# Three 256-column products into one sum, where a 512-column and a 256-column product made two sums

## The chip, the cores and the metric

The kernel runs on one core of a Trainium2 chip. The metric is the device time of one execution in microseconds (us). Engines are named as the profile names them: PE is TensorE's products (MATMUL), PEld its weight loads (LDWEIGHTS), DVE is VectorE, ACT is ScalarE, POOL is GpSimd and SP is SyncE, which issues most DMAs.

## What is computed

One decoder layer on 256 tokens of width 2048, in float32. A projection to seven parts feeds an attention branch and a recurrent branch; each branch is projected and gated, the sum is projected again, and a gated feed-forward part of width 5632 follows. Cut to its matrix products:

```python
def hybrid_layer(x, ...):
    h = rms_norm(x, norm1_w)
    q, k, v, xr, yr, g_att, g_lru = jnp.split(h @ w_in, SPLIT_POINTS, axis=-1)
    att = moba_attention(rms_norm(q), rms_norm(k), v)
    lru = rglru_branch(xr, yr, ...)
    merged = (jax.nn.sigmoid(g_att) * (att @ w_proj_attn)
              + jax.nn.sigmoid(g_lru) * (lru @ w_proj_lru))
    x = x + merged @ w_out
    h2 = rms_norm(x, norm2_w)
    return x + (jax.nn.silu(h2 @ w_ffn_gate) * (h2 @ w_ffn_up)) @ w_ffn_down
```

## The kernel before

All weights together are a list of 292 pieces of 512 rows x 512 columns (1 MB each), used one after the other in the order in which `plan` was filled. SP fetches a piece three ahead of its use (`load`). `split` makes two parts of every piece, each in two halves of 256 rows: ACT rounds it to `w_hi` (L107) and DVE subtracts to get the rest, `w_lo` (L108). There are four buffers of halves for each part, so that two pieces are held at a time, and a half is written again when TensorE has used it for the last time. The left operands (`hT`, `attT`, `lruT`, `merged`, `h2T`, `mid`) are held in two parts in the same way, as [128, part, 4, 256]. A product of x and w is made of three: high by high, high by low, low by high.

A block is 512 columns of one projection, 4 pieces long (11 in the last projection, `fd`). The 12 blocks of q, k and v (48 pieces) keep the activations stationary (`tokens_first`: L648, L649, L650, three products of 512 columns for each 128 rows and half of the tokens, each with its own weight load, though two follow each other with the same stationary operand). The other 244 pieces keep the weights stationary (`features_first`). For each of the 4 groups of 128 rows (k) and 4 groups of 128 columns (f), a block of `w_hi` is loaded and meets both parts of the activations in one product of 512 columns (L661; the two parts lie 1024 elements apart, so the operand is read in two runs of 256), and then a block of `w_lo` is loaded and meets the high part in one of 256 columns (L662). These are pairs of products; there are 16 in a piece and 3904 in all. A block's two sums are two PSUM tiles `acc[g]`, one for each two f; `gather` copies one sum out with ACT (L304) and adds the other with DVE (L305), half a block per piece, and then the work of the block's kind follows (multiplying by the row's 1/rms, gates, residual sums).

The order on each engine is the order of the program: behind each piece `run_due` issues the tasks that are due (`later(delay, ...)` counts in pieces), at most one of them for TensorE. `aux` products of these tasks (attention scores, transposes, recurrent gates) stand between pieces. The last piece of all goes one f at a time, in the order 0, 2, 1, 3, and `last_evac` adds and stores each f behind it.

Of the kernel before, what the change touches and what calls it, by code (L numbers as in the profile page):

```python
# [23 lines left out]
CB = 512          # columns of one block of a projection  # L24
KT = 4            # chunks of 128 rows in one loaded piece of a weight
# [5 lines left out]
# columns of `vecs`, 16 each (feature = column * 128 + partition)  # L31
# [6 lines left out]
def layer(ctx: ExitStack, tc: tile.TileContext, x, xT, vecs, w_in, w_rg_a, w_rg_x,  # L38
# [18 lines left out]
    pieces = []     # (source, first row chunk, first column)  # L57
# [5 lines left out]
    plan = []       # (kind, index, source of the left operand)  # L63
# [28 lines left out]
    def load(n):  # L92
        if n >= len(pieces):
            return
        w, k, c = pieces[n]
        raw[n] = wp.tile([P, KT, CB], F32, name="w_raw", bufs=4)
        src = w[k * P:(k + KT) * P, c:c + CB].rearrange("(k p) n -> p k n", p=P)
        if n == 0:
            return src
        if n > 1:  # L100
            sync.dma_start(raw[n], src)
        else:
            for s in range(0, KT, 2):
                sync.dma_start(raw[n][:, s:s + 2], src[:, s:s + 2])
# [49 lines left out]
    # the first pieces come chunk by chunk, so that TensorE starts early  # L154
# [16 lines left out]
    # identity, distances  # L171
# [17 lines left out]
    def rsqrt_mean(name, ss, n, width, where=small):  # L189
        """(ss / n + EPS) ** -0.5"""  # L190
        r = where.tile([P, width], F32, name=name)
        pool.tensor_scalar(r, ss, 1.0 / n, EPS, op0=OP.mult, op1=OP.add)
        pool.tensor_tensor(r, r, mhalf[:, :width], op=OP.pow)
        return r
# [3 lines left out]
    def rows_of(r):  # L198
        """[token, half] -> [128 times the same, token]: a task for TensorE, then a copy"""
        box = const.tile([P, T], F32, name="rb")  # L200

        def on_pe():
            t = aux()
            for h in range(2):
                pe.transpose(t[:, h * P:(h + 1) * P], r[:, h:h + 1].to_broadcast([P, P]), ident)
            later(1, lambda: act.activation(box, t[:, :T], AF.Copy))
        later(1, on_pe, True)
        return box

# [31 lines left out]
    # softplus(-lambda) = max(-lambda, 0) + 2 atanh(e / (2 + e)), e = exp(-|lambda|)  # L241
# [23 lines left out]
    tasks = []      # [slot, order, on TensorE, function]  # L265
# [20 lines left out]
    def transposed(src):  # L286
        """[token, half, 512 features] -> PSUM [feature, 4, token]"""
        t = aux()
        tv = t.rearrange("p (k h t) -> p k h t", k=KT, h=2)
        for k in range(KT):  # L290
            for h in range(2):
                pe.transpose(tv[:, k, h, :], src[:, h, k * P:(k + 1) * P], ident)  # L292
        return t

    def parts_of(dst, src):
        """dst [128, 2, 4, 256] from src [128, 4, 256]"""
        act.activation(dst[:, 0], src, AF.Copy)
        later(1, lambda: dve.tensor_tensor(dst[:, 1], src, dst[:, 0].bitcast(F32), op=OP.subtract))

    def gather(acc, dst, then):  # L300
        """dst [128, 4, 256] from the two sums of each feature"""
        def half(g):
            d = dst[:, 2 * g:2 * g + 2]
            act.activation(d, acc[g][:, :, 1, :], AF.Copy)  # L304
            dve.tensor_tensor(d, acc[g][:, :, 0, :], d, op=OP.add)  # L305
        later(0, lambda: half(0))
        later(1, lambda: (half(1), then()))
# [55 lines left out]
    def scores(b):  # L363
# [44 lines left out]
        def turn(z, pair):  # L408
            t = aux().rearrange("p (a n) -> p a n", a=2)
            for a in range(2):  # L410
                hd = 2 * pair + a
                # keys of the first half: queries of both halves; keys of the second: queries of it
                pe.transpose(t[:, a, :P], z[:, hd, :P], ident)  # L413
                pe.transpose(t[:, a, P:2 * P], z[:, hd, P:2 * P], ident)  # L414
                pe.transpose(t[:, a, 2 * P:3 * P], z[:, hd, 2 * P:], ident)  # L415

            def after():
                if pair == 0:
                    box["pT"] = arena.tile([P, KT, 3 * P], F32, name="pT", tag="m7")
                act.activation(box["pT"][:, 2 * pair:2 * pair + 2], t[:, :, :3 * P], AF.Copy)  # L420
                if pair == 1:
                    later(0, values, True)
            later(1, after)
# [22 lines left out]
    sg = {}  # L446

    def gate_of(s, delay=1):
        dve.tensor_tensor(s, s, rows(st["rb1"]), op=OP.mult)
        later(delay, lambda: act.activation(s, s, AF.Sigmoid))  # L450

    def ga_done(j, acc):
        if j % 2 == 0:
            sg["pair"] = arena.tile([P, 2, KT, T], F32, name="s", tag=f"m{8 + j // 2}")
        sg[j] = sg["pair"][:, j % 2]
        gather(acc, sg[j], lambda: gate_of(sg[j]))

    def pa_done(j, acc):
        t = feat_tile(f"t{j % 2}", "pa")
        gather(acc, t, lambda: dve.tensor_tensor(sg[j], t, sg[j], op=OP.mult))  # L460

    def gl_done(j, acc):
# [5 lines left out]
        gather(acc, s, lambda: gate_of(s, 2))  # L468

    def pl_done(j, acc):  # L470
        t = feat_tile(f"t{j % 2 * 2}", "pl")

        def then():
            dve.tensor_tensor(t, t, sg["l", j], op=OP.mult)
# [3 lines left out]
        gather(acc, t, then)  # L478

# [1 line left out]
    lru = {}  # L481

    def xr_done(b, acc):
# [12 lines left out]
        def scaled():  # L496
            dve.tensor_tensor(xv, xv, rows(st["rb1"]), op=OP.mult)
            conv(0)
            later(1, lambda: conv(1))
# [37 lines left out]
        def factor(g, at):  # L537
            # 1 - a^2 = tanh(-log a) (1 + a^2)
# [10 lines left out]
        gather(acc, xv, scaled)  # L549

    def yr_done(b, acc):
        s = feat_tile("t2", "yr")

        def then():
            dve.tensor_tensor(s, s, rows(st["rb1"]), op=OP.mult)
            later(2, lambda: act.activation(s, s, AF.Gelu_apprx_tanh))
            later(5, product)
# [5 lines left out]
        gather(acc, s, then)  # L563

# [9 lines left out]
    def add(xb, acc, f):  # L574
        for s in (1, 0):
            dve.tensor_tensor(xb[:, f], acc[f.start // 2][:, f.start % 2:(f.stop - 1) % 2 + 1, s, :],
                              xb[:, f], op=OP.add)

    def wo_done(j, acc):
        xb = res[j]  # L580

        def then():
            add(xb, acc, slice(2, 4))
# [7 lines left out]
        later(0, lambda: add(xb, acc, slice(0, 2)))  # L591
        later(1, then)

# [1 line left out]
    ff = {}  # L595

    def fg_done(j, acc):
        g = feat_tile(f"t{j % 2}", "fg")

        def scaled():  # L600
            s = feat_tile("t2", "fs")
            dve.tensor_tensor(g, g, rows(st["rb2"]), op=OP.mult)
# [6 lines left out]
        gather(acc, g, lambda: later(3 if j == 0 else 0, scaled))  # L609

    def fu_done(j, acc):
        u = feat_tile("t3", "fu")

        def scaled():
            dve.tensor_tensor(u, u, rows(st["rb2"]), op=OP.mult)
# [3 lines left out]
        gather(acc, u, lambda: later(2 if j == 0 else 0, scaled))  # L619

    def fd_done(j, acc):
        xb = res[j]

        def then():
            add(xb, acc, slice(2, 4))
            sync.dma_start(out_rows[:, j * KT:(j + 1) * KT], xb)
        later(0, lambda: add(xb, acc, slice(0, 2)))
        later(1, then)
# [12 lines left out]
    def tokens_first(acc, a, n, first, last):  # L641
        """acc [token, half, column]: the left operand's parts are stationary"""
# [9 lines left out]
    def features_first(acc, a, n, first, last, fs=range(KT)):  # L652
        """acc[g] [column, 2, 2, token]: the weight's parts are stationary; its first part meets both parts
        of the activations in one product, and the two sums are added in the end"""
        for g in range(2):
            mine = [(k, f) for k in range(KT) for f in fs if f // 2 == g]
            for k, f in mine:
                hi, lo = (p[:, k % 2, f * P:(f + 1) * P] for p in parts[n][k // 2])
                o = acc[g][:, f % 2]
                start, stop = first and k == 0, last and k == KT - 1  # L660
                pe.matmul(o, hi, a[:, :, k, :], start=start, stop=False, skip_group_check=True)  # L661
                pe.matmul(o[:, 0, :], lo, a[:, 0, k, :], start=False, stop=stop, skip_group_check=True)  # L662

    for kind, j, n0, count in plan:
# [3 lines left out]
        else:  # L668
            acc = [psum.tile([P, 2, 2, T], F32, name="acc", tag="acc", bufs=3) for g in range(2)]
# [70 lines left out]
```

## Time and profile before

| | |
|---|---|
| median of 3 runs (1688.47 to 1690.04) | 1689.32 us |
| span of the profiled execution, first to last instruction | 1686.6 us |
| PE / PEld busy | 1676.7 / 1455.4 us |
| DVE / ACT busy | 1040.0 / 827.9 us |
| granted TensorE clock, mean | 1.000 |
| DMA, mean over the span | 190 GB/s |

The time that lies around the span is taken as 1689.3 - 1686.6 = 2.7 us; the profiled execution has no other time than its span. A product's duration in the trace reaches from its start to the end of its last result, so that products overlap, and their rhythm has to be read from start to start, or from the busy time of a group divided by its count where products of the group cover its whole stretch.

### The profile page before, as it was taken

To read this page: it belongs to the slowest core of one execution; us is meant where nothing else is said; L and a number is where in the kernel's file an instruction comes from. 1 tells how busy PE (TensorE), PEld (TensorE's weight loads), DVE (VectorE), ACT (ScalarE), POOL (GpSimd) and SP (SyncE) were. 2 spreads that over 40 slices of the span, in tenths; PEclk is the share of its full clock that TensorE was granted. 3 is DMA by queue.
4 is the path that set the end of the run, shared out by engine and by line. 5 is a ranking of instruction groups with operands and counts; after the bars stand their busy time and mean duration, and the time that the engine had idled before them with its cause. 6 is when DMAs were issued, how large, how long until landed. Compare 5 with 4: busy or idle time off the path is not lost.

```text
span 1686.6 us, 22468 instructions
## 1 busy us (share of the span) xinstructions
PE 1676.7 (99%) x9276; PEld 1455.4 (86%) x9276; DVE 1040.0 (62%) x1064; ACT 827.9 (49%) x960; POOL 27.7 (2%) x35
## 2 busy tenths in 40 slices
PE   8999999999999999999999999999999999999999
PEld 6888888888888888888888888888888888888887
DVE  6565656655556867768666656666666666554444
ACT  6544554544445665756445444444444444443332
POOL 0100101000000000000000000000000000000000
PEclk9999999999999999999999999999999999999999
DMA  8554545555555555555557655555556555565662
GB/s 306 190 179 155 177 169 174 170 173 182 190 198 175 187 184 203 187 175 177 198 188 245 216 189 186 200 180 194 192 184 199 181 193 192 184 223 188 213 218 82
DMA packets 166294, 320.30 MB, mean 190 GB/s; under 512 B 5296, under 2 KB 15664, under 8 KB 166192
## 3 DMA queue, kind: packets, MB, share of 16 engines
q1 hardware_dynamic: 165328, 316.51, 55.6%
q0 software_dynamic: 576, 2.10, 0.3%
q8 instruction: 72, 1.18, 0.3%
q10 hardware_dynamic: 288, 0.26, 0.0%
q14 instruction: 30, 0.25, 0.0%
HBM read 314.66 MB, written 4.19 MB: 189 GB/s over the span
## 4 chain that ended last, share of the span: by engine, by line
PE 99%; DMA 0%; ACT 0%; SPq 0%; DVE 0%; issue 0%
PE acc L661 53%; PE acc L662 27%; PE acc L649 5%; PE acc L650 5%; PE acc L648 5%; PE aux L515 1%; PE aux L292 0%; PE aux L372 0%; PE aux L431 0%; DMA xc<-in_xT 0%; PE aux L433 0%; PE aux L371 0%; PE aux L415 0%; PE aux L413 0%; PE aux L414 0%; SPq L158 0%
## 5 line engine op out<-in xcount | busy, mean ns | idle before, releaser
L108 DVE TENSOR_TENSOR w_lo<-w_raw,w_hi 128x1024 fp32r<-128x1024 f32 (+1 forms) x586 | 711.9, 1221 | 575.8 <-ACT w_hi L107 575.7
L107 ACT ACTIVATE w_hi<-w_raw 128x1024 fp32r<-128x1024 f32 (+1 forms) x586 | 619.0, 1058 | 757.0 <-PE acc L661 548.5
L661 PE MATMUL acc<-h2T,w_hi 128*128 128x512 f32 x1408 | 488.9, 392 | 0.0
L662 PE MATMUL acc<-h2T,w_lo 128*128 128x256 f32 x1408 | 394.3, 280 | 0.0
L661 PE MATMUL acc<-hT,w_hi 128*128 128x512 f32 x1024 | 360.9, 397 | 0.0
L661 PEld LDWEIGHTS acc<-h2T,w_hi 128*128 128x128 f32 x1408 | 263.4, 187 | 58.1
L662 PE MATMUL acc<-hT,w_lo 128*128 128x256 f32 x1024 | 286.3, 280 | 0.0
L662 PEld LDWEIGHTS acc<-h2T,w_lo 128*128 128x128 f32 x1408 | 266.1, 189 | 0.0
L661 PE MATMUL acc<-mid,w_hi 128*128 128x512 f32 x704 | 244.1, 391 | 0.0
L661 PEld LDWEIGHTS acc<-hT,w_hi 128*128 128x128 f32 x1024 | 192.1, 188 | 45.2
L662 PE MATMUL acc<-mid,w_lo 128*128 128x256 f32 x704 | 197.1, 280 | 0.0
L662 PEld LDWEIGHTS acc<-hT,w_lo 128*128 128x128 f32 x1024 | 193.2, 189 | 0.3
L648 PE MATMUL acc<-w_hi,hT 128*128 128x512 f32 x384 | 153.9, 401 | 5.5 <-ACT w_hi L107 5.4
L661 PEld LDWEIGHTS acc<-mid,w_hi 128*128 128x128 f32 x704 | 131.6, 187 | 28.9
L649 PE MATMUL acc<-w_lo,hT 128*128 128x512 f32 x384 | 151.0, 393 | 0.8 <-DVE w_lo L108 0.8
L650 PE MATMUL acc<-w_hi,hT 128*128 128x512 f32 x384 | 150.7, 392 | 0.0
L662 PEld LDWEIGHTS acc<-mid,w_lo 128*128 128x128 f32 x704 | 133.1, 189 | 0.0
L648 PEld LDWEIGHTS acc<-w_hi,hT 128*128 128x128 f32 x384 | 72.8, 190 | 20.9 <-ACT w_hi L107 6.5
L661 PE MATMUL acc<-attT,w_hi 128*128 128x512 f32 x256 | 90.5, 399 | 0.0
L661 PE MATMUL acc<-merged,w_hi 128*128 128x512 f32 x256 | 90.5, 399 | 0.0
L661 PE MATMUL acc<-lruT,w_hi 128*128 128x512 f32 x256 | 90.3, 398 | 0.1
L649 PEld LDWEIGHTS acc<-w_lo,hT 128*128 128x128 f32 x384 | 72.7, 189 | 16.5 <-DVE w_lo L108 2.0
(166 smaller groups left out, 1303.8 us busy)
## 6 DMA issues: line engine op xcount, KB each, us to landing
w_raw<-in_w_in SPq DMA_DIRECT2D x110, 1024.0 KB, 5.0
w_raw<-in_w_ffn_gate SPq DMA_DIRECT2D x44, 1024.0 KB, 5.0
w_raw<-in_w_ffn_up SPq DMA_DIRECT2D x44, 1024.0 KB, 5.0
w_raw<-in_w_ffn_down SPq DMA_DIRECT2D x44, 1024.0 KB, 5.0
w_raw<-in_w_proj_attn SPq DMA_DIRECT2D x16, 1024.0 KB, 5.0
w_raw<-in_w_proj_lru SPq DMA_DIRECT2D x16, 1024.0 KB, 4.9
w_raw<-in_w_out SPq DMA_DIRECT2D x16, 1024.0 KB, 5.1
xb<-in_xT SPq DMA_DIRECT2D x4, 512.0 KB, 7.9
```

The costliest lines, as they stand in the source:

```text
L107: act.activation(hi, r, AF.Copy)
L108: dve.tensor_tensor(lo, r, hi.bitcast(F32), op=OP.subtract)
L515: pe.matmul(t[:, n * T:(n + 1) * T], wg[:, i, n, :], u[:, n, :], start=True, stop=True, skip_group_check=True)
L648: pe.matmul(o, ah, hi, start=(first and k == 0), stop=False)
L649: pe.matmul(o, ah, lo, start=False, stop=False)
L650: pe.matmul(o, al, hi, start=False, stop=(last and k == KT - 1))
L661: pe.matmul(o, hi, a[:, :, k, :], start=start, stop=False, skip_group_check=True)
L662: pe.matmul(o[:, 0, :], lo, a[:, 0, k, :], start=False, stop=stop, skip_group_check=True)
```

## The change

`features_first` makes three products of 256 columns for each k and f, all into one sum: `w_hi` by the high part, `w_hi` by the low part, `w_lo` by the high part. Its loops are exchanged: f is outside, k inside. A block's sums fit one PSUM tile `acc` of two banks, and `gather` is gone. In its place `by_rows` reads the tile with one DVE instruction, which multiplies by the row's 1/rms in the same pass; the residual sums take one addition for a block in place of four. Delays of tasks are set for this. In DRAM every weight lies piece by piece, with a partition's 4 x 512 numbers of a piece in one run of 8 KB, where there were four runs of 2 KB in four rows.

```diff
-        src = w[k * P:(k + KT) * P, c:c + CB].rearrange("(k p) n -> p k n", p=P)
+        src = w[k // KT, c // CB]
...
-    def gather(acc, dst, then):
-        """dst [128, 4, 256] from the two sums of each feature"""
-        def half(g):
-            d = dst[:, 2 * g:2 * g + 2]
-            act.activation(d, acc[g][:, :, 1, :], AF.Copy)
-            dve.tensor_tensor(d, acc[g][:, :, 0, :], d, op=OP.add)
-        later(0, lambda: half(0))
-        later(1, lambda: (half(1), then()))
+    def by_rows(acc, dst, r, then, delay=0):
+
+        def fn():
+            dve.tensor_tensor(dst, acc, rows(st[r]), op=OP.mult)
+            then()
+        later(delay, fn)
...
     def add(xb, acc, f):
-        for s in (1, 0):
-            dve.tensor_tensor(xb[:, f], acc[f.start // 2][:, f.start % 2:(f.stop - 1) % 2 + 1, s, :],
-                              xb[:, f], op=OP.add)
+        dve.tensor_tensor(xb[:, f], acc[:, f], xb[:, f], op=OP.add)
...
             later(1, lambda: parts_of(mid[j], u))
-        gather(acc, u, lambda: later(2 if j == 0 else 0, scaled))
+        by_rows(acc, u, "rb2", lambda: later(3, scaled), 1 if j == 0 else 0)
...
-        for g in range(2):
-            mine = [(k, f) for k in range(KT) for f in fs if f // 2 == g]
-            for k, f in mine:
+
+
+        for f in fs:
+            for k in range(KT):
                 hi, lo = (p[:, k % 2, f * P:(f + 1) * P] for p in parts[n][k // 2])
-                o = acc[g][:, f % 2]
-                start, stop = first and k == 0, last and k == KT - 1
-                pe.matmul(o, hi, a[:, :, k, :], start=start, stop=False, skip_group_check=True)
-                pe.matmul(o[:, 0, :], lo, a[:, 0, k, :], start=False, stop=stop, skip_group_check=True)
+                o = acc[:, f, :]
+                start, stop = first and k == 0 and f % 2 == 0, last and k == KT - 1
+                pe.matmul(o, hi, a[:, 0, k, :], start=start, stop=False, skip_group_check=True)
+                pe.matmul(o, hi, a[:, 1, k, :], start=False, stop=False, skip_group_check=True)
+                pe.matmul(o, lo, a[:, 0, k, :], start=False, stop=stop, skip_group_check=True)
...
-            acc = [psum.tile([P, 2, 2, T], F32, name="acc", tag="acc", bufs=3) for g in range(2)]
+            acc = psum.tile([P, KT, T], F32, name="acc", tag="acc", bufs=3)
...
+        if not k.startswith("w_rg"):
+            rows_, cols_ = given[k].shape
+            given[k] = (given[k].reshape(rows_ // (KT * P), KT, P, cols_ // CB, CB)
+                        .transpose(0, 3, 2, 1, 4))
```

Line numbers move: the three products of `features_first` are L648, L649 and L650 of the changed kernel. On TensorE's queue, in a features-first piece of the attention gate's projection where the piece's second half is used for the first time, before (`acc_2222` is the PSUM tile of f = 0 and 1, the numbered `w_hi` and `w_lo` are halves of the piece):

```order
L661 MATMUL acc_2222<-hT_84,w_hi_2302 128x512
L662 MATMUL acc_2222<-hT_84,w_lo_2303 128x256
L661 MATMUL acc_2222<-hT_84,w_hi_2306 128x512
L662 MATMUL acc_2222<-hT_84,w_lo_2307 128x256
L661 MATMUL acc_2222<-hT_84,w_hi_2306 128x512
```

The same place in the changed kernel (`acc_2222` is now the tile of the whole block; the numbers of halves differ):

```order
L648 MATMUL acc_2222<-hT_84,w_hi_2317 128x256
L649 MATMUL acc_2222<-hT_84,w_hi_2317 128x256
L650 MATMUL acc_2222<-hT_84,w_lo_2318 128x256
L648 MATMUL acc_2222<-hT_84,w_hi_2321 128x256
L649 MATMUL acc_2222<-hT_84,w_hi_2321 128x256
L650 MATMUL acc_2222<-hT_84,w_lo_2322 128x256
```

Where two products stood for a k and an f, three stand now, and the second half of the piece's rows is used for the first time after 6 products (of 48), where it was after 8 (of 32). The whole TensorE queue has 3904 rows more.

In the last piece, on TensorE's queue with its waits, the changed kernel has at the end of f = 0 and the beginning of f = 2:

```order
L649 MATMUL acc_16409<-mid_14652,w_hi_16934 128x256
L650 MATMUL acc_16409<-mid_14652,w_lo_16935 128x256
L648 MATMUL acc_16409<-mid_14652,w_hi_16930 128x256 [waits DVE_49]
L649 MATMUL acc_16409<-mid_14652,w_hi_16930 128x256
L650 MATMUL acc_16409<-mid_14652,w_lo_16931 128x256
```

Before, that place read (f = 2 has a tile of its own, and only the third and the fourth f wait for DVE):

```order
L661 MATMUL acc_12940<-mid_11613,w_hi_13325 128x512
L662 MATMUL acc_12940<-mid_11613,w_lo_13326 128x256
L661 MATMUL acc_12941<-mid_11613,w_hi_13321 128x512
L662 MATMUL acc_12941<-mid_11613,w_lo_13322 128x256
L661 MATMUL acc_12941<-mid_11613,w_hi_13321 128x512
```

All four f now lie in one tile, so each of the last three waits for the DVE addition of the f just before it; before, an f waited for the addition of the one two before it.

On DVE, over a gate block and an up block of the feed-forward part, before:

```order
L305 TENSOR_TENSOR fg<-acc,fg 128x512
L298 TENSOR_TENSOR mid<-fu,mid 128x1024
L108 TENSOR_TENSOR w_lo<-w_raw,w_hi 128x1024 x2
L602 TENSOR_TENSOR fg<-fg,rb 128x1024
L108 TENSOR_TENSOR w_lo<-w_raw,w_hi 128x1024 x4
L607 TENSOR_TENSOR fg<-fg,fs 128x1024
L305 TENSOR_TENSOR fu<-acc,fu 128x512
```

The same blocks in the changed kernel:

```order
L303 TENSOR_TENSOR fg<-acc,rb 128x1024
L108 TENSOR_TENSOR w_lo<-w_raw,w_hi 128x1024 x4
L597 TENSOR_TENSOR fg<-fg,fs 128x1024
L298 TENSOR_TENSOR mid<-fu,mid 128x1024
L108 TENSOR_TENSOR w_lo<-w_raw,w_hi 128x1024 x4
L303 TENSOR_TENSOR fu<-acc,rb 128x1024
```

The additions of `gather` (two of 512 numbers a block) are gone, and the product with the row's 1/rms reads PSUM itself.

## Rows read from the trace of the kernel before

**Rows 1.** The page: span, busy times, granted clock in 40 slices, chain by engine.

```profile
span 1686.6 us, 22468 instructions
PE 1676.7 (99%) x9276; PEld 1455.4 (86%) x9276; DVE 1040.0 (62%) x1064; ACT 827.9 (49%) x960; POOL 27.7 (2%) x35
PEclk9999999999999999999999999999999999999999
PE 99%; DMA 0%; ACT 0%; SPq 0%; DVE 0%; issue 0%
```

**Rows 2.** What PE waited for: us in total, times, longest us.

```profile
PE acc L648 <- ACT w_hi L107: 5.4, 1, 5.4
PE acc L649 <- DVE w_lo L108: 0.8, 1, 0.8
```

**Rows 3.** Groups by line, PE: xcount | busy us, mean ns | idle before.

```profile
L661 PE MATMUL acc<-h2T,w_hi 128*128 128x512 f32 x1408 | 488.9, 392 | 0.0
L662 PE MATMUL acc<-h2T,w_lo 128*128 128x256 f32 x1408 | 394.3, 280 | 0.0
L661 PE MATMUL acc<-hT,w_hi 128*128 128x512 f32 x1024 | 360.9, 397 | 0.0
...
L661 PE MATMUL acc<-mid,w_hi 128*128 128x512 f32 x704 | 244.1, 391 | 0.0
...
L661 PE MATMUL acc<-attT,w_hi 128*128 128x512 f32 x256 | 90.5, 399 | 0.0
L661 PE MATMUL acc<-merged,w_hi 128*128 128x512 f32 x256 | 90.5, 399 | 0.0
L661 PE MATMUL acc<-lruT,w_hi 128*128 128x512 f32 x256 | 90.3, 398 | 0.1
```

**Rows 4.** Timeline at 1000 us (feed-forward), PE: start us, duration us.

```profile
999.90 0.39 PE L661 MATMUL acc<-h2T,w_hi 128*128 128x512 f32 x1
1000.13 0.28 PE L662 MATMUL acc<-h2T,w_lo 128*128 128x256 f32 x1
1000.25 0.39 PE L661 MATMUL acc<-h2T,w_hi 128*128 128x512 f32 x1
```

**Rows 5.** Timeline at 76 us (tokens-first), PE: eleven steps of 512 columns.

```profile
76.07 0.39 PE L648 MATMUL acc<-w_hi,hT 128*128 128x512 f32 x1
...
78.56 0.39 PE L650 MATMUL acc<-w_hi,hT 128*128 128x512 f32 x1
```

**Rows 6.** Groups by line, PEld: the weight load of the second product, tokens-first.

```profile
L649 PEld LDWEIGHTS acc<-w_lo,hT 128*128 128x128 f32 x384 | 72.7, 189 | 16.5 <-DVE w_lo L108 2.0
```

**Rows 7.** Timeline at 1000 us, PEld alone: the load for the third product of rows 4.

```profile
1000.13 0.19 PEld L661 LDWEIGHTS acc<-h2T,w_hi 128*128 128x128 f32 x1
```

**Rows 8.** Timeline at 37.5 us: one-column products, and two weight loads behind them.

```profile
37.50 0.50 PE L230 MATMUL aux<-ones,sq 128*128 128x1 f32 x4
...
37.83 0.19 PEld L648 LDWEIGHTS acc<-w_hi,hT 128*128 128x128 f32 x1
37.86 0.49 PE L648 MATMUL acc<-w_hi,hT 128*128 128x512 f32 x1
37.95 0.19 PEld L649 LDWEIGHTS acc<-w_lo,hT 128*128 128x128 f32 x1
```

**Rows 9.** Timeline at 1105 us: a piece's halves are split on ACT and DVE.

```profile
1104.68 1.06 ACT L107 ACTIVATE w_hi<-w_raw 128x1024 fp32r<-128x1024 f32 x1 [0.67 <-PE acc L661]
1106.06 1.06 ACT L107 ACTIVATE w_hi<-w_raw 128x1024 fp32r<-128x1024 f32 x1 [0.33 <-PE acc L661]
...
1107.16 1.22 DVE L108 TENSOR_TENSOR w_lo<-w_raw,w_hi 128x1024 fp32r<-128x1024 f32 x1 [0.16 <-ACT w_hi L107]
```

**Rows 10.** DMA issues of the largest group: count, size, median us to landing.

```profile
w_raw<-in_w_in SPq DMA_DIRECT2D x110, 1024.0 KB, 5.0
```

**Rows 11.** Timeline of the end: last product, its two additions.

```profile
1682.72 0.28 PE L662 MATMUL acc<-mid,w_lo 128*128 128x256 f32 x1
1683.04 0.88 DVE L576 TENSOR_TENSOR xb<-acc,xb 128x256 f32<-128x256 f32 x2 [0.50 <-PE acc L662]
```

More of the change, by code (lines that the diff above doesn't have):

```diff
@@ L448, in gate_of @@
     def gate_of(s, delay=1):
-        dve.tensor_tensor(s, s, rows(st["rb1"]), op=OP.mult)
         later(delay, lambda: act.activation(s, s, AF.Sigmoid))
@@ L455, in ga_done @@
         sg[j] = sg["pair"][:, j % 2]
-        gather(acc, sg[j], lambda: gate_of(sg[j]))
+        by_rows(acc, sg[j], "rb1", lambda: gate_of(sg[j]))
     def pa_done(j, acc):
-        t = feat_tile(f"t{j % 2}", "pa")
-        gather(acc, t, lambda: dve.tensor_tensor(sg[j], t, sg[j], op=OP.mult))
+        later(0, lambda: dve.tensor_tensor(sg[j], acc, sg[j], op=OP.mult))
     def gl_done(j, acc):
@@ L467, in gl_done @@
         sg["l", j] = s
-        gather(acc, s, lambda: gate_of(s, 2))
+        by_rows(acc, s, "rb1", lambda: gate_of(s, 2))
     def pl_done(j, acc):
@@ L473, in then @@
         def then():
-            dve.tensor_tensor(t, t, sg["l", j], op=OP.mult)
+            dve.tensor_tensor(t, acc, sg["l", j], op=OP.mult)
             dve.tensor_tensor(t, t, sg[j], op=OP.add)
@@ L477, in then @@
             later(1, lambda: parts_of(merged[j], t))
-        gather(acc, t, then)
+        later(0, then)
     lru = {}
@@ L496, in scaled @@
         def scaled():
-            dve.tensor_tensor(xv, xv, rows(st["rb1"]), op=OP.mult)
             conv(0)
@@ L548, in scan @@
                 dve.tensor_tensor_scan(hs[:, n], at[:, 0, n], u[:, n], 0.0, OP.mult, OP.add)
-        gather(acc, xv, scaled)
+        by_rows(acc, xv, "rb1", lambda: later(1, scaled))
     def yr_done(b, acc):
@@ L554, in then @@
         def then():
-            dve.tensor_tensor(s, s, rows(st["rb1"]), op=OP.mult)
-            later(2, lambda: act.activation(s, s, AF.Gelu_apprx_tanh))
-            later(5, product)
+            later(3, lambda: act.activation(s, s, AF.Gelu_apprx_tanh))
+            later(6, product)
         def product():
@@ L562, in product @@
             later(1, lambda: halves_of(s, lruT[b][:, 0], lruT[b][:, 1]))
-        gather(acc, s, then)
+        by_rows(acc, s, "rb1", then)
     x1d = dram.tile([P, NB, KT, T], F32, name="x1d")
@@ L582, in then @@
         def then():
-            add(xb, acc, slice(2, 4))
+            add(xb, acc, slice(0, 4))
             pool.dma_start(x1d[:, j], xb)
@@ L590, in parts @@
             square(j, xb, ("t2", "t3", tmp), "2")
-        later(0, lambda: add(xb, acc, slice(0, 2)))
-        later(1, then)
+        later(0, then)
     ff = {}
@@ L601, in scaled @@
             s = feat_tile("t2", "fs")
-            dve.tensor_tensor(g, g, rows(st["rb2"]), op=OP.mult)
             later(1, lambda: act.activation(s, g, AF.Sigmoid))
@@ L608, in silu @@
             ff[j] = g
-        gather(acc, g, lambda: later(3 if j == 0 else 0, scaled))
+        by_rows(acc, g, "rb2", scaled, 4 if j == 0 else 0)
     def fu_done(j, acc):
@@ L614, in scaled @@
         def scaled():
-            dve.tensor_tensor(u, u, rows(st["rb2"]), op=OP.mult)
             dve.tensor_tensor(u, u, ff[j], op=OP.mult)
@@ L624, in then @@
         def then():
-            add(xb, acc, slice(2, 4))
+            add(xb, acc, slice(0, 4))
             sync.dma_start(out_rows[:, j * KT:(j + 1) * KT], xb)
-        later(0, lambda: add(xb, acc, slice(0, 2)))
-        later(1, then)
+        later(0, then)
     def last_evac(acc, f):
```

## The prediction

> **What bounds the kernel now.** I read the page first: TensorE is busy for 1676.7 of 1686.6 us, the chain that ended last is TensorE by 99%, and the granted clock is at full speed, 2.4 GHz, in all 40 slices [rows 1]. A busy TensorE may still wait, so the waits come next: it waited for another engine twice, 6.2 us together, both at the first weights [rows 2]. Then the stream is read from start to start. So the time is the number of products times their rhythm, and no other engine's saving shortens it.
>
> The rhythm of a features-first pair is the busy time of the L661 groups over their counts, since a 512-column product lasts 391 to 399 ns and the next begins before it ends [rows 3]. This gives 244.1 / 704 = 346.7 ns with `mid`, 347.2 with `h2T`, 352.4 with `hT`, and 353 to 354 with `attT`, `merged` and `lruT`. The six groups add up to 1365.2 us for 3904 pairs, 349.7 ns each. A pair's 768 columns at 2.4 GHz are 320 ns. The rest, 26.7 ns in the fastest stage and 29.7 on the mean, is paid for something other than columns. The question is for what.
>
> **The change part by part.** *Products.* Each of 3904 pairs becomes three products of 256 columns: the same 768 columns, one product and one weight load more. The first two of a triple share `w_hi`, but the tokens-first part shows that sharing saves no load: L648 and L649 have the same stationary operand, and L649 has 384 loads for its 384 products [rows 6]. No row shows 256-column products one after another, so the price has to be bounded.
>
> The nearest rows are two. Eleven tokens-first steps of 512 columns took 2.49 us [rows 5], 226 to 227 ns each, 13 ns over the 213.3 of the columns. One such product and its load cost 13 ns; the two of a pair cost 26.7 in the fastest stage. A fixed cost of 13.3 ns for each product with its load explains both (226.7 and 346.7), though the mean number of columns differs, 512 and 384. By it a triple takes 3 x (106.7 + 13.3) = 360 ns, and 3904 x 360 = 1405.4 us, 40.2 more than now. With the mean of today, 14.85 ns for each product, it is 364.6 ns and 1423.2 us, 58.0 more. Which of the rhythms the new sequence falls into can't be read; I take the middle, **+49 us**. With the slow stages' 16.7 to 17 ns a triple takes 370 ns, +79: the upper end of this case.
>
> The other row is the step behind a 256-column product inside a pair: 117 ns, from 1000.13 to 1000.25, where 0.12 is printed [rows 4] and 346.7 less 230 leaves it. Taken as that product's full cost, three are 351 ns, +5 us. I prefer the first reading, because the 512-column step of the pair is then 230, longer than the 227 of tokens-first: the two starts seem to be shifted by 3 ns within a sum that fits.
>
> The Trainium skill (TensorE: Matmul & The Clock Gate, Back-to-back issue gap) gives N / 2.4 + 2.5 ns for one product behind another at full clock. By it a triple would be 327.5 ns and a pair 324.9, so the change would cost 2.6 ns a triple, an estimated 10 us. The trace does not agree with its fixed part here: 227 ns stand where it has 215.8.
>
> *Weight loads.* A load starts when the product before it starts (1000.13 in both [rows 4, 7]), so it hides behind that product if it is short enough. Two loads whose product in between does not hold them back are 0.12 us apart, 37.83 and 37.95 [rows 8]; behind a 256-column product there are 107 ns of columns. So the load path is nearly full and can't give a step much below 112 ns (three are 336, -53 us: the lower end of all). I keep both ends.
>
> *Evacuation.* `gather`'s copies and additions leave ACT and DVE, and so does a separate multiplication. Nothing waited for them, so this gives 0; what hides it is TensorE's stream itself.
>
> *Halves.* With k inside f, the first half of a piece is used until product 42 of 48 (before 24 of 32), so it comes free about 0.7 us later, and the second half is needed after 6 of 48 products, 0.7 us sooner than after 8 of 32. Before, ACT begins a half when it is free, at 1104.68 and 1106.06, and DVE's second `w_lo` ends at 1107.16 + 1.22 = 1108.4 [rows 9]; the piece in use lasts 16 x 0.347 = 5.55 us from 1106.06, to 1111.6. The 3 us of room cover both shifts: 0. Where DVE has more beside it the room is smaller, but this is also where DVE loses most.
>
> *Layout in DRAM.* A piece lands 5.0 us after its issue [rows 10] and is asked for three pieces ahead, 16 us: 0 for longer runs. At the start, where two waits make 6.2 us [rows 2], the first piece still comes in 2 KB runs by row chunks, and these waits end by ACT and DVE: 0, at best 1 us less.
>
> *The last piece.* Each of the last three f now waits for the addition just before it. Today the addition starts 0.32 us behind the last product's start (1682.72 to 1683.04), and two take 0.88 us [rows 11]. One takes 0.44, and with a load that is no longer hidden, 0.11, the step is 0.87 instead of 0.12: 0.75 x 3 = 2.2 us more, less 0.44 for the one addition fewer at the end, **+1.8 us**. If these waits were nothing, it would be -0.4.
>
> **Sum.** 1686.6 + 49 + 1.8 = 1737.4 us of span; with the 2.7 us around it, which tie the span to the median, **1740 us**, 3.0% slower.
>
> **The rivals.**
> *The third product is hidden* (15%): a 256-column step is really 117 ns and the load is what sets it. For it speaks the step inside the pair [rows 4], against it the fit of one constant to two sums. 1365.2 becomes 3904 x 351 = 1370.3: 1689.3 + 5.1 + 1.8 = 1696 us. The Trainium skill's formula above lands near this case, at 1701 us by that estimate.
> *Faster* (14%): the 512-column product pays for reading its operand in two runs, and what is over the columns grows with them. Then contiguous products step by 226.7 / 512 ns a column, 113.3 ns for 256, a triple is 340 ns, 3904 of them 1327.4 us: 1689.3 - 37.8 + 1.8 = 1653 us. It decides from a step below 349.7 / 3 = 116.6 ns on. For it speaks the 230 of the pair against tokens-first's 227; against it, that a pair would be 340 at best, and no stage is below 346.7 [rows 3].
> *The load is saved after all* (5%): the second `w_hi` stays in place. Two loads per triple as now, so the rhythm does not change: 1691 us. Rows 6 speak against it.
> *TensorE's instructions don't come fast enough* (6%): A product and its load are two instructions; today they are taken every 173 ns on the mean of a pair (346.7 / 2), and then it would be every 120. Each 10 ns too late cost 3904 x 30 ns = 117 us; at 130 ns, 3904 x 390 = 1522.6, so 1849 us. Against it: four one-column products with their loads passed between 37.50 and 37.86 [rows 8], 90 ns each, though only four.
>
> **How the numbers follow.** The likeliest case, a fixed cost per product, has 60%; its own range is 1731 to 1771 us (from +40 and +79, each with 1.8). The range of 8 in 10 takes in this case, the hidden third product and the saved load, which is 60 + 15 + 5: **1690 to 1778 us**, the top with some room for rhythms slower than today's slowest. About 0.2%, 3.4 us, is what a measurement of this kernel can tell from no change. Faster by more: the one faster case, 14%. Within: the saved load and a part of the hidden case, 7%. Slower: the rest, 79%.
>
> **What would show it.** TensorE's busy groups by line: L648 to L650 of the changed kernel with 3904 rows each, and a step from start to start of 120 to 123 ns; the `mid` stage (704 triples) at 253 to 260 us, where it is 244.1 now. If that stage is at 247 the third product is hidden, at 239 or less the two-run read was the cost. PEld must count 3904 loads more. Waits of TensorE must stay at the start, with three new ones near the end, of some 0.7 us each, ended by the additions. It is wrong altogether if TensorE shows waits for `w_hi` or `w_lo` in the middle, since then the halves, not the rhythm, set the time.

## The result, and the profile after the change

The changed kernel takes 1732.68 us (1732.25 to 1734.44, 4 runs) beside 1688.89 us for the kernel before in the same session: a ratio of 1.0261 (1.0246 to 1.0275), so 43.8 us or 2.6% slower. The forecast was 1740 us. The changed kernel's page answers to [rows 1]:

```profile
span 1730.8 us, 30009 instructions
PE 1720.0 (99%) x13180; PEld 1667.8 (96%) x13180; DVE 946.3 (55%) x947; ACT 754.7 (44%) x868; POOL 27.7 (2%) x35
PEclk9999999999999999999999999999999999999999
PE 99%; DMA 0%; SPq 0%; DVE 0%; ACT 0%; issue 0%
```

DVE lost 93.7 us of work, ACT 73.2, and the DMA packets fell to a third (54707 where e2 below shows 166294). All of that went where the chain is not: the chain that ended last is still TensorE's by 99%. TensorE has 3904 products and 3904 loads more (13180 against 9276 in both), at the same granted clock, full speed in all slices, and is busy 43.3 us longer. The span grew by 44.2.

What the changed kernel's TensorE waited for (total us, times, longest us) answers to [rows 2]:

```profile
PE acc L636 <- ACT w_hi L107: 5.4, 1, 5.4
PE acc L648 <- DVE xb L569: 1.6, 3, 0.5
PE acc L637 <- DVE w_lo L108: 0.8, 1, 0.8
```

The two waits at the first weights are as they were. Three new ones stand at the end, 0.5 us each where the forecast had some 0.7, and nothing in the middle waits for a half of a piece. So the 44 us are neither waits nor clock; they lie in the rhythm. The timeline of the changed kernel at 1000 us, PE and PEld, answers to [rows 4, 7]:

```profile
999.83 0.28 PE L648 MATMUL acc<-h2T,w_hi 128*128 128x256 f32 x1
999.95 0.28 PE L649 MATMUL acc<-h2T,w_hi 128*128 128x256 f32 x1
1000.07 0.28 PE L650 MATMUL acc<-h2T,w_lo 128*128 128x256 f32 x1
...
1001.27 0.28 PE L648 MATMUL acc<-h2T,w_hi 128*128 128x256 f32 x1
```

Twelve steps from 999.83 to 1001.27 are 1.44 us, 120 ns each; the first two, printed, are 0.12 each. The groups by line of the changed kernel (xcount | busy us, mean ns | idle before) answer to [rows 3]:

```profile
L648 PE MATMUL acc<-mid,w_hi 128*128 128x256 f32 x704 | 199.5, 283 | 1.6 <-DVE xb L569 1.6
...
L649 PEld LDWEIGHTS acc<-h2T,w_hi 128*128 128x128 f32 x1408 | 270.3, 192 | 0.0
```

Beware of these rows: a product now lasts 283 ns and comes back every 360, so the busy time of a line no longer covers its stage, as L661's did. L649 has its own 1408 loads, though L648 has just loaded the same weights. For a stage's time I take all of TensorE's products that read one tile, over the whole span (busy us, then the number of products). In the changed kernel, for `hT` (with the tokens-first part), `attT`, `h2T` and `mid`:

```profile
0.00:1900.00 1900.00, 645.18 (x4224) 1.00 0.48 169
0.00:1900.00 1900.00, 92.32 (x768) 1.00 0.48 169
0.00:1900.00 1900.00, 507.50 (x4224) 1.00 0.48 169
0.00:1900.00 1900.00, 254.35 (x2112) 1.00 0.48 169
```

The same four in the kernel before:

```profile
0.00:1900.00 1900.00, 635.49 (x3200) 1.00 0.50 169
0.00:1900.00 1900.00, 90.62 (x512) 1.00 0.50 169
0.00:1900.00 1900.00, 489.28 (x2816) 1.00 0.50 169
0.00:1900.00 1900.00, 244.22 (x1408) 1.00 0.50 169
```

`lruT` and `merged` go as `attT` does, from 90.56 and 90.62 to 92.32. Less the tail of the last product (0.283 - 0.12 = 0.16 us), `attT` gives 92.16 / 256 = 360.0 ns a triple, against 353.4 a pair. The six rows grow by 9.7 + 1.7 + 1.8 + 1.7 + 18.2 + 10.1 = 43.2 us. With the 1.6 us of new waits that is 44.8, and an end that is 0.5 us shorter makes it 44.3. The changed kernel's end, PE and DVE, answers to [rows 11]:

```profile
1725.21 0.28 PE L650 MATMUL acc<-mid,w_lo 128*128 128x256 f32 x1
1725.53 0.42 DVE L569 TENSOR_TENSOR xb<-acc,xb 128x256 f32<-128x256 f32 x1 [1.78 <-PE acc L650]
1726.00 0.39 PE L648 MATMUL acc<-mid,w_hi 128*128 128x256 f32 x1 [0.52 <-DVE xb L569]
1726.23 0.28 PE L649 MATMUL acc<-mid,w_hi 128*128 128x256 f32 x1
...
1727.41 0.28 PE L650 MATMUL acc<-mid,w_lo 128*128 128x256 f32 x1
1727.73 0.42 DVE L569 TENSOR_TENSOR xb<-acc,xb 128x256 f32<-128x256 f32 x1 [1.78 <-PE acc L650]
```

From 1725.21 to 1726.00 a step takes 0.79 us, and the next 0.23, in place of 0.12 each: 0.78 us for each of three waits. Behind the last product one addition ends 0.74 us after its start, where two took 1.20.

### The profile page after: what moved, and what is told of

Same layout as the page of the kernel before. It is cut to its first block, busy times and chain, and to the rows that moved or that the text cites. A ratio compares the mean times of both kernels' runs of the same rounds, so it can differ in the third digit from the quotient of the medians.

```text
span 1730.8 us, 30009 instructions
## 1 busy us (share of the span) xinstructions
PE 1720.0 (99%) x13180; PEld 1667.8 (96%) x13180; DVE 946.3 (55%) x947; ACT 754.7 (44%) x868; POOL 27.7 (2%) x35
## 2 busy tenths in 40 slices
DMA packets 54707, 320.79 MB, mean 185 GB/s; under 512 B 5296, under 2 KB 15664, under 8 KB 17456
## 4 chain that ended last, share of the span: by engine, by line
PE 99%; DMA 0%; SPq 0%; DVE 0%; ACT 0%; issue 0%
PE acc L648 27%; PE acc L649 27%; PE acc L650 27%; PE acc L637 5%; PE acc L638 5%; PE acc L636 5%; PE aux L510 1%; PE aux L292 0%; PE aux L370 0%; PE aux L429 0%; DMA xc<-in_xT 0%; PE aux L369 0%; PE aux L431 0%; PE aux L411 0%; PE aux L413 0%; PE aux L412 0%
## 5 line engine op out<-in xcount | busy, mean ns | idle before, releaser
L108 DVE TENSOR_TENSOR w_lo<-w_raw,w_hi 128x1024 fp32r<-128x1024 f32 (+1 forms) x586 | 692.5, 1218 | 599.4 <-ACT w_hi L107 599.4
L107 ACT ACTIVATE w_hi<-w_raw 128x1024 fp32r<-128x1024 f32 (+1 forms) x586 | 591.6, 1050 | 938.4 <-PE acc L649 741.2
L648 PE MATMUL acc<-h2T,w_hi 128*128 128x256 f32 x1408 | 398.6, 283 | 0.0
L649 PE MATMUL acc<-h2T,w_hi 128*128 128x256 f32 x1408 | 398.5, 283 | 0.0
L650 PE MATMUL acc<-h2T,w_lo 128*128 128x256 f32 x1408 | 398.5, 283 | 0.0
L648 PE MATMUL acc<-hT,w_hi 128*128 128x256 f32 x1024 | 291.9, 285 | 0.0
L650 PE MATMUL acc<-hT,w_lo 128*128 128x256 f32 x1024 | 289.8, 283 | 0.0
L649 PE MATMUL acc<-hT,w_hi 128*128 128x256 f32 x1024 | 289.8, 283 | 0.0
L649 PEld LDWEIGHTS acc<-h2T,w_hi 128*128 128x128 f32 x1408 | 270.3, 192 | 0.0
L648 PEld LDWEIGHTS acc<-h2T,w_hi 128*128 128x128 f32 x1408 | 270.3, 192 | 0.0
L650 PEld LDWEIGHTS acc<-h2T,w_lo 128*128 128x128 f32 x1408 | 270.3, 192 | 0.0
L648 PE MATMUL acc<-mid,w_hi 128*128 128x256 f32 x704 | 199.5, 283 | 1.6 <-DVE xb L569 1.6
L649 PE MATMUL acc<-mid,w_hi 128*128 128x256 f32 x704 | 199.2, 283 | 0.0
L650 PE MATMUL acc<-mid,w_lo 128*128 128x256 f32 x704 | 199.2, 283 | 0.0
L649 PEld LDWEIGHTS acc<-hT,w_hi 128*128 128x128 f32 x1024 | 196.5, 192 | 0.3
L648 PEld LDWEIGHTS acc<-hT,w_hi 128*128 128x128 f32 x1024 | 196.5, 192 | 0.3
L650 PEld LDWEIGHTS acc<-hT,w_lo 128*128 128x128 f32 x1024 | 196.5, 192 | 0.0
L648 PEld LDWEIGHTS acc<-mid,w_hi 128*128 128x128 f32 x704 | 135.1, 192 | 2.2 <-DVE xb L569 2.2
L649 PEld LDWEIGHTS acc<-mid,w_hi 128*128 128x128 f32 x704 | 135.1, 192 | 0.0
```

What stands on the lines that cost most here:

```text
L107: act.activation(hi, r, AF.Copy)
L108: dve.tensor_tensor(lo, r, hi.bitcast(F32), op=OP.subtract)
L648: pe.matmul(o, hi, a[:, 0, k, :], start=start, stop=False, skip_group_check=True)
L649: pe.matmul(o, hi, a[:, 1, k, :], start=False, stop=False, skip_group_check=True)
L650: pe.matmul(o, lo, a[:, 0, k, :], start=False, stop=stop, skip_group_check=True)
```

## The experiments

The theory was the forecast's: each product with its load costs some 13 ns beside its columns. Rivals were a cost of reading the operand in two runs, a cost of the load alone, and the other parts of the change. Each quoted text names its theories itself.

**e1_three**: only the split of the products, in the kernel before; sums, evacuation, order and layout stay.

```diff
-                pe.matmul(o, hi, a[:, :, k, :], start=start, stop=False, skip_group_check=True)
+                pe.matmul(o[:, 0, :], hi, a[:, 0, k, :], start=start, stop=False, skip_group_check=True)
+                pe.matmul(o[:, 1, :], hi, a[:, 1, k, :], start=False, stop=stop, skip_group_check=True)
```

> The kernel before with one edit: the 512-column product of a pair becomes two of 256 columns, into the same two sums as before; evacuation, loop order, tiles and DRAM layout are those of before. Theory A (each product with its load costs a fixed 13.3 ns beside its columns): triples of 360 ns, 3904 x 360 = 1405 us in place of 1365, total 1729 us (1725 to 1733), step 120 ns everywhere. Rival B (the time comes from the new order: f outside, one sum in one place of PSUM, one tile for a block): steps near 116.7 ns, total within 5 us of 1689.

It took 1731.93 us beside 1688.25, a ratio of 1.0232 (1.0182 to 1.0283), within theory A's 1725 to 1733 us. TensorE's products with `h2T` and with `mid` in e1_three:

```profile
0.00:1900.00 1900.00, 507.50 (x4224) 1.00 0.51 169
0.00:1900.00 1900.00, 253.60 (x2112) 1.00 0.51 169
```

`h2T` is that of the full change to the last digit; `mid` lacks the 0.75 us that the exposed loads of the last piece add. So the split alone makes the loss, and ACT's and DVE's `gather`, which e1_three still has (DVE 1041.2 us, as before), is worth nothing.

**e2_layout**: only the layout in DRAM, in the kernel before.

```diff
-        src = w[k * P:(k + KT) * P, c:c + CB].rearrange("(k p) n -> p k n", p=P)
+        src = w[k // KT, c // CB]
```

> The kernel before with the weights piece by piece in DRAM and nothing else. Theory A: the transfers are covered, 1689 us within 2 us, though a third of the packets. Rival: longer runs bring the first pieces sooner, so that the start is up to 2 us shorter; or the other layout disturbs the SBUF writes and shows in the rhythm (then more than 3 us either way).

1689.36 us, a ratio of 1.0002 (0.9975 to 1.0029). The page's DMA line of the kernel before, then of e2_layout:

```profile
DMA packets 166294, 320.30 MB, mean 190 GB/s; under 512 B 5296, under 2 KB 15664, under 8 KB 166192
```

```profile
DMA packets 54678, 320.30 MB, mean 190 GB/s; under 512 B 5296, under 2 KB 15664, under 8 KB 17456
```

Two thirds of the packets go, a piece lands in 4.8 us where it took 5.0 [rows 10], and the time stays: the transfer was hidden.

**e3_contig**: the kernel before with the two parts of the left operand beside each other, so that a 512-column product reads one run.

```diff
-        return arena.tile([P, 2, KT, T], F32R, name=name, tag=tag)
+        return arena.tile([P, KT, 2, T], F32R, name=name, tag=tag).rearrange("p k s t -> p s k t")
```

> The kernel before with the two parts of the activations side by side for each k, so that the 512-column product reads one run of 512 and not two of 256. Theory A1 (fixed 13.3 ns per product; the slow stages of before, 353 ns a pair, come from the two-run operand): 346.7 ns a pair in all stages, 3904 x 346.7 = 1353.5, so about 12 us less, 1677 us. Rival A2 (the slow rhythm comes from mixing 512 and 256 columns): stages at 353 remain, 1689 us within 4 us. Rival C (reading two runs costs 3.3 ns a pair even in the fast stages): 343 ns a pair, 1663 us.

1688.06 us, a ratio of 0.9981 (0.9959 to 1.0003). TensorE's timeline of e3_contig at 450 us, in the `attT` stage:

```profile
449.85 0.40 PE L661 MATMUL acc<-attT,w_hi 128*128 128x512 f32 x1
450.09 0.28 PE L662 MATMUL acc<-attT,w_lo 128*128 128x256 f32 x1
450.20 0.40 PE L661 MATMUL acc<-attT,w_hi 128*128 128x512 f32 x1
...
450.91 0.40 PE L661 MATMUL acc<-attT,w_hi 128*128 128x512 f32 x1
```

Three pairs in 1.06 us, 353 ns, as before, and with `mid` the products take 244.22 us in both kernels. In these pairs the read in two runs costs nothing, and theory A1's 1677 us did not come; rival A2's stages at 353 ns stayed. With it falls the mechanism of the forecast's "faster" rival, and one explanation of the slow stages.

**e4_load64**: the changed kernel, with only 64 of the 128 weight columns in the third product.

```diff
-                pe.matmul(o, lo, a[:, 0, k, :], start=False, stop=stop, skip_group_check=True)
+                pe.matmul(o[:64], lo[:, :64], a[:, 0, k, :], start=False, stop=stop, skip_group_check=True)
```

> The changed kernel, with the third product using 64 of its 128 weight columns (half of the low part of the weights is left out of the result). Same number of products, same columns streamed, a load half as long. Theory A-product (13.3 ns belong to a product, whatever it loads): steps stay 120 ns, 1733 us. Theory A-load (13.3 ns are time that the load takes from the stream, by its 128 columns): the step of the product behind or with the short load falls by 6 to 7 ns, 26 us less in all, 1707 us. Rival D (120 ns is the rate of the load path, not of the products): the shortened step falls to 110 or less, 39 us or more saved, 1694 us or less.

One run took 1693.72 us. TensorE's products with `attT` in e4_load64, and the group of its short loads with `h2T`:

```profile
0.00:1900.00 1900.00, 89.76 (x768) 1.00 0.48 169
```

```profile
L650 PEld LDWEIGHTS acc<-h2T,w_lo 128*64 128x64 f32 x1408 | 192.9, 137 | 0.0
```

89.60 / 256 is 350.0 ns a triple, 10 less, with the same number of products and of columns read through. So theory A-product's 1733 us falls, and the cost beside the columns seems to be partly the load's. That is not quite shown: the short product also writes 64 partitions of PSUM in place of 128, and no run separates the two. The total is the one that rival D named, but its step is not: D asked for one step of 110 ns or less, and here all three are a little shorter than 120, 116.7 on the mean. The 39 us given back bring the kernel near 1689 by chance, not because the third product came free.

**e5_sizes**: the changed kernel with another size in each stage. The second product of q, k and v loads 64 columns, the third product loads 96 with `attT` and 32 with `lruT`, is cut into two of 128 columns with `h2T`, and reads 192 columns with `mid`.

```diff
-                pe.matmul(o, ah, lo, start=False, stop=False)
+                pe.matmul(o[:64], ah[:, :64], lo, start=False, stop=False)
...
+                elif kind in ("fg", "fu"):
+                    pe.matmul(o[:, :P], lo, full[:, :P], start=False, stop=False, skip_group_check=True)
+                    pe.matmul(o[:, P:], lo, full[:, P:], start=False, stop=stop, skip_group_check=True)
```

> The changed kernel with one size changed in each stage, read stage by stage (parts of the result are left out by it). Theory S (a load takes time out of the stream, 13.3 ns with 128 weight columns and 10 ns less with 64, whatever is streamed) against theory L (behind a 256-column product the step is the rate of the load path, 120 ns; with a shorter load it is the columns and 3.3 ns). q, k, v: second product loads 64 columns, streams 512: S three steps of 670 ns, L 680 as before. attT: third product loads 96: S between 350 and 360 a triple, L 350 if the load's time goes with its columns. lruT: third loads 32: S 347 to 350, L 350. h2T: third product in two of 128 columns, each with a full load: S 240 + 2 x 66.7 = 373 ns, L 480. mid: third product streams 192 of 256 columns, full load: S 333 ns, L 360 as before.

One run took 1869.9 us. TensorE's timeline of e5_sizes at 1000 us, with `h2T`:

```profile
999.79 0.33 PE L648 MATMUL acc<-h2T,w_hi 128*128 128x256 f32 x1
999.96 0.28 PE L649 MATMUL acc<-h2T,w_hi 128*128 128x256 f32 x1
1000.08 0.22 PE L656 MATMUL acc<-h2T,w_lo 128*128 128x128 f32 x1
1000.14 0.28 PE L657 MATMUL acc<-h2T,w_lo 128*128 128x128 f32 x1
1000.25 0.33 PE L648 MATMUL acc<-h2T,w_hi 128*128 128x256 f32 x1
```

A 128-column product follows another after 0.06 us (its columns are 53 ns), but the next two steps are 0.11 and 0.17: the time saved is given back behind the loads. Between 1000 and 1600 us 5182 products start, 115.8 ns each, though their columns are 80 ns on the mean (192 x 0.4167). So the columns do not set the pace here; that the loads do, one with each product, is an inference that no run tests. The short loads of e5_sizes, with `attT` and with `lruT`:

```profile
L652 PEld LDWEIGHTS acc<-attT,w_lo 128*96 128x96 f32 x256 | 41.7, 163 | 0.0
L654 PEld LDWEIGHTS acc<-lruT,w_lo 128*32 128x32 f32 x256 | 28.7, 112 | 0.0
```

Loads of 128, 96, 64 and 32 columns last 192, 163, 137 and 112 ns, in order of size, but the triples do not follow them: with 96 columns loaded the triple is 356.0 ns, with 32 it is 353.3, and with 64, in e4_load64, 350.0. The short load in q, k and v saved nothing: three products took 690 ns there, where they took 680. `mid` came to 349 ns. Neither of the two sizes of theory, a cost in proportion to the columns loaded or a bound by the load alone, gives all of these.

**e6_bf16**: the kernel before, with `w_lo` of the features-first products and its operand read as bfloat16, so that its load is shorter.

```diff
-                pe.matmul(o[:, 0, :], lo, a[:, 0, k, :], start=False, stop=stop, skip_group_check=True)
+                pe.matmul(o[:, 0, :], lo, a[:, 0, k, :].bitcast(BF16)[:, 1::2], start=False, stop=stop,
+                          skip_group_check=True)
```

> The kernel before, with the low part of the weights in bfloat16 in the features-first blocks, multiplied with the upper two bytes of the activations' high part (read with a step of two). If a two-byte load takes as little from the stream as the 64-column load did, a pair falls from 349.7 to 337 or 340 ns, 38 to 50 us less in all, 1639 to 1651 us. If the cost does not depend on the type, 1689 us. If the step of two slows the read, the 256-column step is 220 ns or more and the time over 2000 us.

1739.93 us, a ratio of 1.0309 (1.0292 to 1.0326): none of these. The timeline of e6_bf16 at 1000.5 us, PE and PEld:

```profile
1000.54 0.10 PEld L665 LDWEIGHTS <-w_lo 128*128 128x128 bf16 x1 [0.16 <-issue]
1000.54 0.29 PE L665 MATMUL acc<-h2T,w_lo 128*128 128x256 bf16 x1
1000.54 0.20 PEld L664 LDWEIGHTS acc<-h2T,w_hi 128*128 128x128 f32 x1
1000.58 0.48 PE L664 MATMUL acc<-h2T,w_hi 128*128 128x512 f32 x1
1000.90 0.10 PEld L665 LDWEIGHTS <-w_lo 128*128 128x128 bf16 x1 [0.16 <-issue]
```

The bfloat16 load is half as long (0.10 against 0.19) but starts 0.32 us behind the start of the 512-column product, together with its own product, where a four-byte load starts with the product before it [rows 4, 7]. A pair takes 0.36 us. The short load was bought with its cover, and the read with a step of two is not told apart from it, so this run says nothing of the load's share.

**e7_bf16after**: the same in the changed kernel's third product.

> The changed kernel with the same low part in bfloat16 as in the run beside it. If a two-byte load costs less, a triple falls from 360 to about 350 ns and the time to 1694 us; if the cost does not depend on the type, 360 ns and 1733 us. If the fixed cost is one of four-byte streams, and the product's own step falls to 107 to 110 ns without the load's change, the sum is the same 347 to 350, and the steps beside it tell which.

One run took 1760.93 us, a triple 367 ns (94.12 us of products with `attT`): missed. In its timeline, too, the bfloat16 load starts with its own product, at 1000.09 us, and the two four-byte loads behind it only at 1000.10 and 1000.22.

**e8_eights**: the kernel before, in each half block all eight 512-column products first and then the eight of 256.

```diff
-            for k, f in mine:
+            for s, k, f in [(s, k, f) for s in range(2) for k, f in mine]:
```

> The kernel before with its pairs taken apart: in each half block of a piece first the eight 512-column products, then the eight 256-column ones (same products, loads, sums and tiles). Theory: a product's step depends on its columns and its load, 226.7 and 120 ns, and the slow rhythm of before (353 ns a pair in four stages) comes from 512 and 256 columns in turn: 346.7 ns a pair in every stage, 12 us less than before, 1677 us. Rival: the slow rhythm follows from where a stage happens to start and stays: 1689 us within 3 us, with other stages at 353. If the order matters the other way, an even 350 or more.

1689.18 us, a ratio of 1.0000 (0.9985 to 1.0016). TensorE's timeline of e8_eights at 1001 us, eight products to a row:

```profile
1001.12 1.11 PE L663 MATMUL acc<-h2T,w_lo 128*128 128x256 f32 x8
1002.07 2.00 PE L661 MATMUL acc<-h2T,w_hi 128*128 128x512 f32 x8
1003.91 0.28 PE L663 MATMUL acc<-h2T,w_lo 128*128 128x256 f32 x1
```

Eight short products take 0.95 us, 119 ns each, and eight long ones 1.84, 230 each: 349 together. A 256-column product costs near 120 ns in a kernel that has nothing else of the change, and the 117 ns inside a pair [rows 4] were no saving. The theory's 346.7 ns and 1677 us did not come: 512-column products take 230 ns here where the theory had 226.7. The rival has the total, but no stage is left at 353; what was seen is nearest to the last case, an even 350. The rhythm is the same in all stages: `attT` falls from 90.62 to 89.55 us, `h2T` rises from 489.28 to 492.26.

**e9_twos**: the same in groups of two and two.

```diff
-            for k, f in mine:
+            for s, k, f in [(s, k, f) for k in range(KT) for s in range(2) for kk, f in mine if kk == k]:
```

> As the run beside it, but in twos: for each k two 512-column products (two f), then the two 256-column ones. Theory: fewer changes between sizes than before, so at most as slow; between 1677 and 1689 us. Rival (where a stage starts decides): 1689 us within 3 us. If the two runs differ, the number of changes between the sizes is what counts.

1685.79 us, a ratio of 0.9985 (0.9977 to 0.9994). TensorE's products with `hT` and `h2T` in e9_twos:

```profile
0.00:1900.00 1900.00, 633.07 (x3200) 1.00 0.51 169
0.00:1900.00 1900.00, 491.09 (x2816) 1.00 0.51 169
```

It gains 2.4 us with `hT` and 3.6 in the three small stages, and loses 3.0 with `h2T` and `mid`. It is the fastest version run, 2.6 us below the kernel before: its interval leaves out a ratio of 1, but the gain is less than the 0.2% that was called a difference.

**e10_tail**: the changed kernel, with a PSUM tile of its own for each of the last piece's four f.

```diff
-                o = acc[:, f, :]
+                o = acc[f] if isinstance(acc, list) else acc[:, f, :]
```

> The changed kernel with a PSUM tile of its own for each of the four f of the last block. Theory: the three waits of TensorE for the addition, 0.80 us from start to start in place of 0.12, go: the stage with mid ends 2.0 us sooner, the span falls from 1730.8 to 1728.8 us. Rival: the waits are for the engine's order and stay, or another wait takes their place: 1730.8 us within 0.5.

One run took 1731.28 us. TensorE's waits in e10_tail:

```profile
PE acc L636 <- ACT w_hi L107: 6.4, 2, 5.6
PE acc L637 <- DVE w_lo L108: 0.8, 1, 0.8
```

The three waits are gone. TensorE's products with `mid` take 253.60 us here, as in e1_three, so the stage gives back 254.35 + 1.6 - 253.60 = 2.35 us; the span fell by only 1.2, since this run lost 1.0 us at the first weights.

**e11_qkv**: the kernel before, with the second product of the tokens-first part, which the change leaves alone, split into two of 256.

```diff
-                pe.matmul(o, ah, lo, start=False, stop=False)
+                for c in (slice(0, CB // 2), slice(CB // 2, CB)):
+                    pe.matmul(o[:, c], ah, lo[:, c], start=False, stop=False)
```

> The kernel before with one edit in the tokens-first part (q, k, v): the second of its three 512-column products becomes two of 256 columns; here the activations are the stationary operand and the weights stream. Theory (a product with its load costs 13.3 ns beside its columns, whichever operand streams): 384 products more, 680 ns becomes 226.7 + 240 + 226.7 = 693 ns for a group, 5.1 us more in all, 1693 to 1694 us. Rival (the cost belongs to the features-first stream, where DVE and ACT write the stationary halves beside it): no change, 1688 us. Rival (256-column steps are as short as 113.3 or 117 ns between 512-column ones): 680 to 687 ns, 0 to 2.7 us more.

1693.52 us, a ratio of 1.0029 (0.9994 to 1.0065), too close to none for the run times to tell. The trace tells it: TensorE's products with `hT` rise from 635.49 to 640.30 us, for 384 products more, 12.5 ns each. Three undisturbed groups at 100 us, from start to start, give 697 ns each in place of 680, 17 ns. So an extra product costs 12 to 17 ns here too, with the roles of weights and features exchanged.

## Why the prediction was right, and where its size was off

**Products.** Right in kind: a fixed cost of each product with its load, no room for the third product, no load saved. The forecast's first figure, 360 ns a triple, is what every stage shows. What was mis-sized is the term as I took it, +49 us, the middle between 360 and 364.6 ns. The upper figure carried the slow stages' rhythm (353 ns a pair) into the new sequence; with three equal products it is gone. Measured, the six rows grow by 43.2 us, 42.4 without the exposed loads (`mid` of e1_three), which is 6.6 less than 49. The reading with 13.3 ns had 40.2; the 2.2 us between lie on the side of before, since the L661 groups [rows 3] put a pair at 349.7 ns on the mean, and 1405.4 - 42.4 leaves 349.1.

That one constant of 13.3 ns fits both sizes was in part luck. I took the pair's 230 ns for a 227 with its start shifted by 3 ns. In e8_eights 512-column products that follow one another still take 230, 16.7 over their columns, and a long and a short one together 349, not 346.7. What carried over is the short product's part: with full loads it steps by 119 to 120 ns in e1_three, e8_eights and the changed kernel. The 112 ns that I gave the load path as its least step come from no row: in e5_sizes products with a full load began every 115.8 ns, and in the rows under Open every 0.11 us.

The Trainium skill (TensorE: Matmul & The Clock Gate, Back-to-back issue gap) would have a 256-column step at 109 ns by its formula, which the section itself calls the gap of an isolated product, without a budget for weight loads. The measured 120.0 decides against it for these products with a load each, which are float32r (the type of the two parts; the profile prints f32).

**The last piece.** Predicted +2.2 for three waits and -0.44 for one addition: measured 2.35 (e10_tail) and -0.46. **Evacuation, halves, layout, start**: each put at nothing, and each at nothing, by the list of waits, e1_three and e2_layout. DVE, busy for 55%, still has room for the wider product that reads PSUM.

What is left of the 7.3 us by which the forecast was too high is 0.8: the median lies 1.9 us over the span, not 2.7. On record each run's time, that of profiled ones too, lies 1.7 to 1.8 us over its own span; the 2.7 set the median of three runs against the span of one that was faster. Three slips moved nothing: by the skill's formula a pair is 325.0 ns and the change 2.5 a triple, the upper end of the likeliest case is 1770 us, and at 120 ns a product a first half comes free 0.9 us later, not 0.7.

**The rivals.** The hidden third product fell by `mid` at 253.60 us in e1_three where it asked for 247; the two-run read by e3_contig; the saved load by 1408 loads of L649. TensorE's instructions came fast enough: 3335 products began between 1000 and 1400 us, 119.9 ns each, and in e5_sizes they came every 115.8.

**Open.** Where in the machine the 13.3 ns arise. Against a cost of the product alone stands e4_load64, with its narrower output as the reservation; that the cost follows the columns loaded is refuted by e5_sizes. Nor is it a price of every product with a load. The attention scores are plain float32 products, with a load of 128 columns each. TensorE's timeline of the changed kernel at 82.8 us, two products to a row:

```profile
82.77 0.38 PE L369 MATMUL aux<-kT,qT 128*128 128x128 f32 x2
82.99 0.60 PE L370 MATMUL aux<-kT,qT 128*128 128x256 f32 x2
83.42 0.38 PE L369 MATMUL aux<-kT,qT 128*128 128x128 f32 x2
```

Products of 128 columns step by 0.11 us and those of 256 by 0.215, twice as much for twice the columns: nothing near 13 ns stands beside them. No run changed the type of the big products to plain float32, so what the type has to do with it stays open. Open too is why the kernel before runs at 353 ns a pair in some stages and 347 in others: the two-run read is out (e3_contig), and regular groups remove the difference (e8_eights, e9_twos) without naming it.

## What to carry to other kernels

Where TensorE is busy throughout, price a rewrite by its products and loads as well as by its columns, and read that price from start to start: one more float32r product with its load cost 10.9 ns a triple here even though no column was added, and 93.7 us of work taken from DVE bought nothing. Shape the products as large as they go before saving on evacuation. If sums that are finished one by one lie in one PSUM tile, look at the last piece, where nothing covers the wait (0.78 us each).

## What was not expected of the hardware

A bfloat16 weight load behind a four-byte product wasn't hidden in e6_bf16: it started with its own product, and a pair took 362 ns in place of 347 to 353. A load of a quarter of the weight columns, though shorter (112 and 137 ns), saved less than one of half (6.7 and 10 ns a triple). And products of unequal length alternating ran at two rhythms, 347 and 353 ns, while the same products in equal groups ran at 349 everywhere.
